# One decoder layer on one core: the attention's instructions in source order on every engine, and its output kept transposed up to W_o

## The chip, the cores and the metric

One core of a Trainium2 chip runs one program, from the inputs in HBM to the output in HBM. The metric is the device time of one execution in microseconds. TensorE (PE) multiplies, VectorE (DVE), ScalarE (ACT) and GpSimd (POOL) work on tiles, SyncE (SP) asks for transfers; each engine takes its own list of instructions, and semaphores hold one engine until another, or a transfer, is done.

## What is computed

One decoder layer over 1,024 rows of 1,024 columns, in float32. The mixer has two groups of eight heads, and their normed outputs go through W_o:

```python
z = hn @ w_in                                   # u, v, q, six k/v parts, gates
oa = u * (causal w_s applied to rms(v) per chunk of 128 + b_s)      # gMLP
o  = g0 * softmax(q kc) vc + g1 * softmax(q ks over 16 blocks) vs \
   + g2 * softmax(q kw in a window of 512) vw                       # NSA
h += concat([rmsnorm(oa), rmsnorm(o)]) @ w_o
h += hier_moe(rmsnorm(h))                       # 16 experts, 2 of 4 in the best group
h += (p @ w_ple_proj) * sigmoid(rmsnorm(h) @ w_ple_gate)
out = rmsnorm(h)
```

`rmsnorm(o)` divides each row of 512 numbers by its own root mean square; a factor per row may be applied before W_o or after it.

## The kernel before

The program runs through four stages. Up to about 230 us the projections of z are made; from there to about 617 us the attention runs; then come the routing and the experts, to 1,057 us; and then the last stage (PLE: the gate `pg`, the projection `pe`, the final norm). Products in full precision are made in three matmuls from a high and a low part of each operand (`th`/`tl`, `ph`/`pl`, `wh`/`wl`).

**The attention** is a loop over 132 slots; a slot is one tile of 128 keys for four heads and one block of 128 rows. `trans(s+1)` transposes the four probability tiles `P` of the next slot (L644), ACT copies them as `ph` (L650), DVE takes the rest as `pl` (L652). `run_later()` runs what was put off with `self.later(n, ...)`, above all the exponentials of a score bank (`exps`, L580). Then come matmuls of other work; then `score()` makes the scores of a coming bank (`S`, L565, two banks of PSUM), and DVE their row maxima (`nm`, L570); then `mult(s)` adds two matmuls to `O` (L669, L670). POOL scales `P` with the softmax's factor (L604) ahead of the transposes.

**The work between** is a generator: seven matmuls a slot of the last 96 products of `u` (L265) until the pool `late` is open, and after that about three a slot of W_o (`prod`, L771). When a group of 48 matmuls for two tiles of `u` is done, `evac_u` (L225 to L256) passes each tile through gelu, the mask product and a norm: ACT, POOL, DVE, ACT, POOL, DVE, ACT, POOL, and a store to `oa_scr` that POOL asks for (L255). `load_wo` (L740 to L749) brings 128 rows of W_o: two loads that SP asks for, `hi` on POOL (L748), `lo` on DVE (L749). The last four chunks of W_o pass through the one buffer each of `hT` and `hg`.

**What sets the order.** A scheduler lays out the program's instructions on each engine up to the line `self.manual.enter_context(tc.manual_schedule())`; after it they stand in the order in which the code issues them. In the kernel before that line stands behind the third `next(att)`, which runs the whole loop of slots, and the other work is handed to the scheduler with this:

```python
with self.tc.high_priority(offset=-100000), self.tc.issue_after(anchor[0].ins):
    while n < left:
        if next(work, None) is None:
            break
```

**The output of a block.** When a block of rows and four heads is through, ACT copies `O` (L674), PE transposes it in four pieces (L689), and DVE adds the two halves to `ob` (L690). When all eight heads are in, `attended` norms the block: the square on ACT, a factor of two small steps on POOL, and the scaling on DVE (L883). `half` transposes `ob` again for W_o in four pieces (L755).

Of the kernel before, what the change touches and what calls it, by code (L numbers as in the profile page):

```python
# [19 lines left out]
T = 1024  # L20
# [52 lines left out]
class K:  # L73
# [24 lines left out]
    def consts(self, pool):  # L98
# [6 lines left out]
        nc.vector.memset(self.neg_half, -0.5)  # L105
        self.idf = c[:, C_ID:C_ID + 128]
# [295 lines left out]
    def attention(self, blocks, done, work, count):  # L402
# [253 lines left out]
        def mult(s):  # L656
# [14 lines left out]
            if last:  # L671
                def copy(o=O[0]):
                    oe = sb.tile([128, 4, 128], F32, name="oe")
                    AC.activation(oe, o.rearrange("p (h q) -> p h q", h=4), AF.Copy)  # L674
                    if s + 1 < len(slots):
                        self.later(1, lambda: self.pq.append(lambda: out(i, g, oe)))
                    return oe

                if s + 1 < len(slots):
                    self.later(1, copy)  # L680
                else:
                    return i, g, copy()

        def out(i, g, oe):
            if g == 0:
                ob[i] = sb.tile([128, 512], F32, name="ob")
            tp = ps.tile([128, 4, 128], F32, name="tp")
# [16 lines left out]
        for s in range(len(slots)):  # L704
# [28 lines left out]
        out(*evac)  # L733
# [25 lines left out]
    def half(self, o):  # L759
# [3 lines left out]
        return th, tl  # L763

# [11 lines left out]
    def work(self, W, blocks):  # L776
# [31 lines left out]

        def add(X, n, p):
# [4 lines left out]
            V.tensor_add(X["h1"][:, s], p, X["h1"][:, s])  # L814
# [12 lines left out]
        def rest(X, nxt):  # L827
            trans_h(X, 1)
            load_h(nxt)
            self.logits(X["i"], X["hT"], X["hg"][:, T:T + 1])  # L830
# [9 lines left out]
        for n, i in enumerate(blocks[:-1]):  # L840
# [9 lines left out]
            X["ob"] = self.ready[i]  # L850
            trans(X, "ob")
            p = [None, None]
            for k in range(2):
                p[k] = ps.tile([128, 512], F32, name="wo", tag="fl")
                yield from self.prod(p[k], X["toa"], 0, k, True, False)
            trans(N, "oa")
            for k in range(2):
                yield from self.prod(p[k], X["tob"], 1, k, False, True)
                add(X, k, p[k])
# [13 lines left out]
    def attended(self, i, ob):  # L873
        def norm():
            sq = self.small.tile([128, 4], F32, name="sq")
            jk = self.sb.tile([128, 512], F32, name="junk", tag="ph")
            self.nc.scalar.activation(jk, ob, AF.Square, accum_out=sq[:, 0:1])
            self.rstd(sq[:, 1:2], sq[:, 0:1], 512)
            self.obs = sq

        def scale(self=self):
            sq = self.obs
            self.nc.vector.tensor_scalar(ob, ob, sq[:, 1:2], None, op0=OP.mult)  # L883

        def ready():
            self.ready[i] = ob

        norm()
        scale()
        ready()  # L890
# [36 lines left out]
    def tail(self, att, moe, work, i):  # L927
# [14 lines left out]
        for r in work:  # L942
            if r is None:
# [12 lines left out]
        tt = self.half(ob)  # L956
# [955 lines left out]
```

## Time and profile before

| | us |
|---|---|
| median of 3 runs | 1183.36 (1180.6 to 1183.68) |
| the profiled execution: its time | 1184.59 |
| its span, first to last instruction | 1182.9 |
| PE busy in the span | 1128.9 |
| DVE, ACT, POOL busy | 761.8, 664.6, 368.5 |

The profile is one execution. The 1.7 us between its time and its span lie around the span. Lines in it are those of the kernel before.

### The profile page before, as it was taken

To read this page: it belongs to the slowest core of one execution; us is meant where nothing else is said; L and a number is where in the kernel's file an instruction comes from. 1 tells how busy PE (TensorE), PEld (TensorE's weight loads), DVE (VectorE), ACT (ScalarE), POOL (GpSimd) and SP (SyncE) were. 2 spreads that over 40 slices of the span, in tenths; PEclk is the share of its full clock that TensorE was granted. 3 is DMA by queue.
4 is the path that set the end of the run, shared out by engine and by line. 5 is a ranking of instruction groups with operands and counts; after the bars stand their busy time and mean duration, and the time that the engine had idled before them with its cause. 6 is when DMAs were issued, how large, how long until landed. Compare 5 with 4: busy or idle time off the path is not lost. (4 is left out here: it accounts for less than half of the span.)

```text
span 1182.9 us, 17701 instructions
## 1 busy us (share of the span) xinstructions
PE 1128.9 (95%) x5969; PEld 862.6 (73%) x5969; DVE 761.8 (64%) x1264; ACT 664.6 (56%) x1295; POOL 368.5 (31%) x566
## 2 busy tenths in 40 slices
PE   7999999899899999999999989999999999997996
PEld 5798778777688888887775566766667776655885
DVE  4461144467877687767756568876777787646764
ACT  5562154467577777675643357665675665444433
POOL 1562242357533534433321120121112110012542
PEclk9999999999899999999999999999999999998999
DMA  7685241422530311330257797799768994674561
GB/s 271 203 214 145 66 136 59 155 70 69 192 125 5 108 63 42 98 116 5 79 200 257 290 333 252 248 366 416 284 217 293 410 362 162 197 273 171 187 215 70
DMA packets 75839, 219.54 MB, mean 186 GB/s; under 512 B 12777, under 2 KB 20329, under 8 KB 71137
## 3 DMA queue, kind: packets, MB, share of 16 engines
q1 hardware_dynamic: 63200, 177.68, 43.1%
q0 software_dynamic: 7792, 27.77, 7.4%
q10 hardware_dynamic: 4752, 12.93, 2.8%
q8 instruction: 48, 0.79, 0.3%
q14 instruction: 47, 0.38, 0.1%
HBM read 247.44 MB, written 40.11 MB: 243 GB/s over the span
## 5 line engine op out<-in xcount | busy, mean ns | idle before, releaser
L1413 DVE TENSOR_TENSOR wl<-ra,wh 128x1024 fp32r<-128x1024 f32 x192 | 232.1, 1237 | 54.6 <-ACT wh L1412 38.9
L1412 ACT ACTIVATE wh<-ra 128x1024 fp32r<-128x1024 f32 x176 | 180.3, 1056 | 68.5 <-PE y L91 41.0
L265 PE MATMUL z<-w,xh 128*128 128x512 f32 (+1 forms) x576 | 171.1, 379 | 8.1 <-ACT w L84 7.7
L604 POOL TENSOR_SCALAR P<-P,f 128x384 f32<-128x384 f32 (+3 forms) x188 | 105.1, 579 | 104.9 <-DVE f L625 61.9
L580 ACT ACTIVATE P<-S,nm 128x256 f32<-128x256 f32 (+3 forms) x192 | 105.3, 555 | 48.3 <-DVE nm L570 44.5
L265 PEld LDWEIGHTS z<-w,xh 128*128 128x128 f32 x576 | 105.1, 190 | 27.3 <-ACT w L84 7.7
L652 DVE TENSOR_TENSOR pl<-tp,ph 128x512 fp32r<-128x512 f32 x132 | 89.8, 685 | 39.0 <-ACT ph L650 38.3
L1410 POOL TENSOR_SCALAR wh<-ra 128x1024 fp32r<-128x1024 f32 x16 | 23.7, 1482 | 287.7 <-PE y L91 277.2
L89 PE MATMUL gu<-wh,mxh 128*128 128x512 f32 x256 | 108.3, 423 | 4.8 <-ACT wh L1412 4.8
L570 DVE TENSOR_REDUCE nm<-S 128x1 f32<-128x384 f32 (+3 forms) x148 | 91.6, 627 | 30.7 <-PE S L569 18.1
L265 PE MATMUL z<-w,xl 128*128 128x512 f32 (+1 forms) x288 | 109.0, 379 | 0.9 <-DVE xl L82 0.9
L90 PE MATMUL gu<-wl,mxh 128*128 128x512 f32 x256 | 101.7, 397 | 1.5 <-DVE wl L1413 1.5
L650 ACT ACTIVATE ph<-tp 128x512 fp32r<-128x512 f32 x132 | 78.2, 600 | 42.8 <-PE tp L644 42.2
L91 PE MATMUL gu<-wh,mxl 128*128 128x512 f32 x256 | 101.6, 397 | 0.0
L565 PE MATMUL S<-kT,qT 128*128 128x384 f32 (+3 forms) x384 | 92.6, 349 | 8.8 <-ACT P L580 6.6
L771 PE MATMUL wo<-wo,th 128*128 128x512 f32 x256 | 90.1, 425 | 0.0
L644 PE MATMUL tp<-c,P 128*128 128x128 f32 x528 | 83.5, 275 | 0.4 <-POOL P L604 0.4
L565 PEld LDWEIGHTS S<-kT,qT 128*128 128x128 f32 x384 | 62.9, 195 | 18.6 <-ACT P L580 9.4
L644 PEld LDWEIGHTS tp<-c,P 128*128 128x128 f32 x528 | 65.5, 142 | 12.3 <-POOL P L604 0.7
L89 PEld LDWEIGHTS gu<-wh,mxh 128*128 128x128 f32 x256 | 48.6, 190 | 30.0 <-ACT wh L1412 15.6
L265 PEld LDWEIGHTS z<-w,xl 128*128 128x128 f32 x288 | 54.7, 190 | 11.2 <-DVE xl L82 2.1
L670 PE MATMUL O<-pl,V 128*128 128x512 f32 x132 | 57.1, 433 | 1.0 <-DVE pl L652 1.0
(371 smaller groups left out, 2393.7 us busy)
## 6 DMA issues: line engine op xcount, KB each, us to landing
ra<-in_moe_w_gate SPq DMA_DIRECT2D x32, 1024.0 KB
ra<-in_moe_w_up SPq DMA_DIRECT2D x32, 1024.0 KB
ra<-in_moe_w_down SPq DMA_DIRECT2D x32, 1024.0 KB
rq<-in_moe_w_gate SPq DMA_DIRECT2D x40, 512.0 KB
rq<-in_moe_w_up SPq DMA_DIRECT2D x40, 512.0 KB
rq<-in_moe_w_down SPq DMA_DIRECT2D x40, 512.0 KB
y_scr<-yo ACTq DMA_DIRECT2D x19, 512.0 KB
wraw<-in_w_in SPq DMA_DIRECT2D x32, 256.0 KB
```

What stands on the lines that cost most here:

```text
L89: mm(out, xh, wh, start=first, stop=False)
L90: mm(out, xh, wl, start=False, stop=False)
L91: mm(out, xl, wh, start=False, stop=last)
L265: self.nc.tensor.matmul(p[:, :n], x, w, start=(cc == 0 and j == 0), stop=(cc == 7 and j == 2))
L565: PE.matmul(S[:, x], qT[i, g][:, h0 + x, a], kk, start=(x + a == 0), stop=(x == hp - 1 and a == 1 and not (dm or wm)))
L570: V.tensor_reduce(u["nm"][:, h0:h0 + hp, k], S, axis=AX.X, op=OP.max, negate=True)
L580: AC.activation(u["P"][k][:, h], S[:, x], AF.Exp, bias=u["nm"][:, h, k:k + 1], accum_out=u["l"][:, h, k:k + 1])
L604: e.tensor_scalar(P, P, f[:, h, k:k + 1], 1.0, op0=OP.mult, op1=OP.mult)
L644: anchor[0] = PE.transpose(tp[:, h], u["P"][k][:, h, kb * 128:(kb + 1) * 128], self.idf)
L771: self.nc.tensor.matmul(p, x, w[:, s], start=first and k + a == 0, stop=last and k == 3 and a == 2)
L1412: AC.activation(hi, w, AF.Copy)
L1413: V.tensor_tensor(lo, w, raw(hi), op=OP.subtract)
```

## The change

1. `tc.manual_schedule()` is entered ahead of the third `next(att)`, and the priority and the anchor are gone. The loop of slots with its other work then stands in the order of the code on all five engines.
2. `O` stays transposed. ACT copies half of it (64 partitions, L685 of the changed kernel), and DVE makes two sums of 64x256 (L687); the four transposes of `O`, the reduction and the four transposes of `ob` are gone. The norm is taken from the square of the transposed block by four matmuls with a column of ones (`norm_t`, `norm_sum`), and its factor is applied after W_o (`add`); the part from `oa` is added on its own (`add_a`).
3. Some steps are put off by a slot (`later`), and the tail calls `tick` more often.
4. In the last stage the gather of the first rows is asked for first, all projections stand ahead of the first transposes, and the other gathers wait for the first rows. The experts' last store is one transfer on ACT's queue.

```diff
@@ mult, out
             if last:
-                def copy(o=O[0]):
-                    oe = sb.tile([128, 4, 128], F32, name="oe")
-                    AC.activation(oe, o.rearrange("p (h q) -> p h q", h=4), AF.Copy)
-                    if s + 1 < len(slots):
-                        self.later(1, lambda: self.pq.append(lambda: out(i, g, oe)))
-                    return oe
...
+                f = lambda o=O[0]: out(i, g, o.rearrange("p (h q) -> p h q", h=4))
                 if s + 1 < len(slots):
-                    self.later(1, copy)
+                    self.later(1, f)
...
-            for h in range(4):
-                PE.transpose(tp[:, h], oe[:, h], self.idf)
-            V.tensor_reduce(ob[i][:, g * 256:(g + 1) * 256].rearrange("p (h d) -> p h d", h=4),
-                            tp.rearrange("p h (a d) -> p h d a", a=2), axis=AX.X, op=OP.add)
+            oe = sb.tile([64, 4, 128], F32, name="oe")
+            AC.activation(oe, o[64:128], AF.Copy)
+            for k in range(2):
+                V.tensor_tensor(ob[i][k * 64:(k + 1) * 64, 2 * g:2 * g + 2], o[0:64, k:4:2], oe[:, k:4:2], op=OP.add)
@@ the loop of slots
-            with self.tc.high_priority(offset=-100000), self.tc.issue_after(anchor[0].ins):
-                while n < left:
-                    if next(work, None) is None:
-                        break
-                    count[0] -= 1
-                    n += 1
+            while n < left:
+                if next(work, None) is None:
+                    break
+                count[0] -= 1
+                n += 1
@@ the norm
+    def norm_t(self, dst, jk, o, tag):
+        self.nc.scalar.activation(jk, o.rearrange("p c q -> p (c q)"), AF.Square)
+        return lambda: self.norm_sum(dst, jk, tag)
+
+    def norm_sum(self, dst, jk, tag):
+        nc = self.nc
+        r = self.ps.tile([128, 512], F32, name="nt", tag=tag)
+        for c in range(4):
+            nc.tensor.matmul(r[:, 0:1], jk[:, c * 128:(c + 1) * 128], self.one, start=(c == 0), stop=(c == 3))
+        nc.vector.tensor_scalar(dst, r[:, 0:1], 1.0 / 512, EPS, op0=OP.mult, op1=OP.add)
+        nc.gpsimd.tensor_tensor(dst, dst, self.neg_half, op=OP.pow)
@@ the W_o work
-            V.tensor_add(X["h1"][:, s], p, X["h1"][:, s])
+            V.scalar_tensor_tensor(X["h1"][:, s], p, X["rb"], X["h1"][:, s], op0=OP.mult, op1=OP.add)
...
-            X["ob"] = self.ready[i]
-            trans(X, "ob")
-            p = [None, None]
+            X["ob"], X["rb"] = self.ready[i]
+            X["tob"] = self.half_t(X["ob"])
...
                 if k == 0:
-                    trans_h(X, 0)
+                    self.later(1, lambda X=X: trans_h(X, 0))
                 else:
-                    rest(X, N)
+                    self.later(1, *rest(X, N))
@@ mixer
             self.open_late = open_late
+            self.manual.enter_context(tc.manual_schedule())
             next(att)
-            self.manual.enter_context(tc.manual_schedule())
@@ last stage
             load_h(tiles[0], nc.sync)
+            load_y(0)
...
-            for q in range(4):
+            for q in range(NP):
                 proj(q)
-            for c in range(1, 3):
-                part(c)
-
+
+                if q < 4:
+                    part(q + 1)
+                if q >= 4:
+                    AC.activation(*late.pop(0), AF.Copy)
+                if q == 3:
+                    add_y(0)
+            trans(tiles[0])
+
+            G.tensor_copy(sb.tile([128, 8], F32, name="sq")[:, 0:1], tiles[0]["y"][1][:, 0:1])
             load_h(tiles[1], G)
```

The order on DVE where the second group of `u` is through and the last four chunks of W_o come in (`wo_3042`, `wo_3051`, `wo6_3060`, `wo7_3069`; `pl`, `nm` and `f` belong to slots). Before, from the middle of it:

```order
L749 SCALAR_TENSOR_TENSOR wo_3051<-hT_3052,par_71,wo_3051 128x512
L570 TENSOR_REDUCE nm_3357<-S_3440 128x1
L749 SCALAR_TENSOR_TENSOR wo_3051<-hg_3056,par_71,wo_3051 128x512
L652 TENSOR_TENSOR pl_3284<-tp_3278,ph_3283 128x512
L608 RECIPROCAL f0_3457<-l_3358 128x4
L652 TENSOR_TENSOR pl_3304<-tp_3298,ph_3303 128x512
L609 TENSOR_TENSOR f_3456<-f0_3457,gates_85 128x4
L749 SCALAR_TENSOR_TENSOR wo6_3060<-hT_3061,par_71,wo6_3060 128x512
L570 TENSOR_REDUCE nm_3472<-S_3474 128x1
L652 TENSOR_TENSOR pl_3324<-tp_3318,ph_3323 128x512
L570 TENSOR_REDUCE nm_3472<-S_3479 128x1
L749 SCALAR_TENSOR_TENSOR wo6_3060<-hg_3065,par_71,wo6_3060 128x512
```

And now, from the first of its eight `lo` steps on (L744 is L749 of before, L572 is L570):

```order
L744 SCALAR_TENSOR_TENSOR wo_3042<-hT_3043,par_71,wo_3042 128x512
L744 SCALAR_TENSOR_TENSOR wo_3042<-hg_3047,par_71,wo_3042 128x512
L744 SCALAR_TENSOR_TENSOR wo_3051<-hT_3052,par_71,wo_3051 128x512
L744 SCALAR_TENSOR_TENSOR wo_3051<-hg_3056,par_71,wo_3051 128x512
L744 SCALAR_TENSOR_TENSOR wo6_3060<-hT_3061,par_71,wo6_3060 128x512
L744 SCALAR_TENSOR_TENSOR wo6_3060<-hg_3065,par_71,wo6_3060 128x512
L744 SCALAR_TENSOR_TENSOR wo7_3069<-hT_3070,par_71,wo7_3069 128x512
L744 SCALAR_TENSOR_TENSOR wo7_3069<-hg_3074,par_71,wo7_3069 128x512
L1111 TENSOR_TENSOR rt_3080<-rt_3080,par_71 128x160
L82 TENSOR_TENSOR tl_3086<-tp4_3087,th_3085 128x512
L82 TENSOR_TENSOR tl_3100<-ob_2621,th_3099 128x512
L572 TENSOR_REDUCE nm_2959<-S_3106 128x1
```

Before, steps of slots stand between any two chunks of W_o; now the eight steps of four chunks, the router's weights and two `tl` stand in a row, and the first `nm` of a slot behind them.

The order on POOL at the same place: `sv` and `ev` belong to `evac_u`, P is scaled for the slots. Before:

```order
L95 TENSOR_SCALAR sv_3013<-sv_3013 128x1
L96 TENSOR_TENSOR sv_3013<-sv_3013,neg_half_73 128x1
L254 TENSOR_SCALAR ev_2999<-ev_2999,sv_3013 128x512
L255 DMA oa_scr_65<-ev_2999 128x512
L244 TENSOR_TENSOR e_3020<-ev_3001 128x512
L247 TENSOR_TENSOR ev_3001<-ev_3001,M_3011 128x512
L604 TENSOR_SCALAR P_2270<-P_2270,f_2977 128x384 x4
L95 TENSOR_SCALAR sv_3026<-sv_3026 128x1
L96 TENSOR_TENSOR sv_3026<-sv_3026,neg_half_73 128x1
L254 TENSOR_SCALAR ev_3001<-ev_3001,sv_3026 128x512
L255 DMA oa_scr_65<-ev_3001 128x512
L506 TENSOR_TENSOR Pc_3156<-Pc_3156,lc_3190 128x2x4x64
```

And now (L606 is L604 of before, L257 is L255, L743 is L748):

```order
L95 TENSOR_SCALAR sv_3013<-sv_3013 128x1
L96 TENSOR_TENSOR sv_3013<-sv_3013,neg_half_73 128x1
L256 TENSOR_SCALAR ev_2999<-ev_2999,sv_3013 128x512
L257 DMA oa_scr_65<-ev_2999 128x512
L246 TENSOR_TENSOR e_3020<-ev_3001 128x512
L249 TENSOR_TENSOR ev_3001<-ev_3001,M_3011 128x512
L95 TENSOR_SCALAR sv_3026<-sv_3026 128x1
L96 TENSOR_TENSOR sv_3026<-sv_3026,neg_half_73 128x1
L256 TENSOR_SCALAR ev_3001<-ev_3001,sv_3026 128x512
L257 DMA oa_scr_65<-ev_3001 128x512
L743 TENSOR_SCALAR wo_3042<-hT_3043,par_71 128x512
L743 TENSOR_SCALAR wo_3042<-hg_3047,par_71 128x512
```

Before, P is scaled between the steps of two tiles; now the steps of the second tile begin behind the store of the first, and eight `hi` steps follow (the first two are shown), ahead of the next scaling of P.

The order on PE at that place. Before, ahead of the first products with W_o:

```order
L569 MATMUL S<-mb,idb 128x128
L755 MATMUL tp_3087<-c,oa 128x128 x4
L755 MATMUL tp_3101<-c,ob 128x128
L644 MATMUL tp<-c,P 128x128 x4
L755 MATMUL tp_3101<-c,ob 128x128 x3
L565 MATMUL S<-kT,qT 128x512 x2
L569 LDWEIGHTS idb
L569 MATMUL S<-mb,idb 128x128
L565 MATMUL S<-kT,qT 128x512 x2
L569 LDWEIGHTS idb
L569 MATMUL S<-mb,idb 128x128
L771 MATMUL wo<-wo,th 128x512 x2
```

And now, from the row behind the last product of `u` on (L786 is L771 of before, L567 is L565, L646 is L644):

```order
L750 MATMUL tp_3087<-c,oa 128x128 x4
L786 MATMUL wo<-wo,th 128x512 x2
L567 MATMUL S<-kT,qT 128x512 x2
L571 LDWEIGHTS idb
L571 MATMUL S<-mb,idb 128x128
L671 MATMUL O<-ph,V 128x512
L672 MATMUL O<-pl,V 128x512
L646 MATMUL tp<-c,P 128x128 x4
L485 LDWEIGHTS idb
L485 MATMUL S<-mc,idb 128x512
L489 MATMUL S<-kcT,qT 128x64 x16
L786 MATMUL wo<-wo,tl 128x512
```

Now the first two products with `th` stand ahead of one bank of scores, and the first product with `tl` ahead of all scores that follow, where before six banks of scores (the last two are shown) stood ahead of the products.

## Rows read from the trace of the kernel before

**Rows 1.** the page, part 1: busy time, share, instructions of each engine
```profile
PE 1128.9 (95%) x5969; PEld 862.6 (73%) x5969; DVE 761.8 (64%) x1264; ACT 664.6 (56%) x1295; POOL 368.5 (31%) x566
```

**Rows 2.** stretches of the core: us, busy time of each engine, granted clock, DMA share, GB/s
```profile
240.00:270.00 30.00, 29.02 (x171) 23.82 (x171) 20.70 (x41) 18.78 (x51) 18.26 (x31) 0.97 0.19 59
270.00:300.00 30.00, 28.85 (x170) 22.82 (x169) 23.62 (x42) 21.57 (x54) 21.67 (x32) 1.00 0.27 88
300.00:330.00 30.00, 27.72 (x147) 21.22 (x148) 23.58 (x43) 18.24 (x43) 16.87 (x25) 0.89 0.52 174
303.20:310.00 6.80, 6.35 (x23) 4.67 (x23) 4.62 (x9) 4.23 (x11) 5.06 (x7) 0.50 0.99 295
330.00:360.00 30.00, 30.00 (x199) 25.76 (x198) 22.62 (x48) 20.05 (x50) 10.99 (x16) 1.00 0.35 111
540.00:570.00 30.00, 29.03 (x170) 22.68 (x169) 23.88 (x48) 19.06 (x51) 11.01 (x16) 1.00 0.14 45
```

**Rows 3.** the page, part 5: PE's scores, with the idle time before them
```profile
L565 PE MATMUL S<-kT,qT 128*128 128x384 f32 (+3 forms) x384 | 92.6, 349 | 8.8 <-ACT P L580 6.6
```

**Rows 4.** timeline of POOL, one tile of u: start, us, instruction [idle before]
```profile
294.35 1.03 POOL L244 TENSOR_TENSOR e<-ev 128x512 f32<-128x512 f32 x1 [0.29 <-ACT ev L232]
296.38 1.27 POOL L247 TENSOR_TENSOR ev<-ev,M 128x512 f32<-128x512 f32 x1 [0.99 <-DVE e L245]
297.77 2.73 POOL L604 TENSOR_SCALAR P<-P,f 128x384 f32<-128x384 f32 x4
300.59 0.19 POOL L95 TENSOR_SCALAR sv<-sv 128x1 f32<-128x1 f32 x1
302.51 0.61 POOL L255 DMA_DIRECT2D oa_scr<-ev  x1 [0.30 <-POOL ev L254]
```

**Rows 5.** groups by line and form, 200 to 640 us: busy, mean ns
```profile
L248 DVE SCALAR_TENSOR_TENSOR ev<-e,ev 128x512 f32<-128x512 f32 x4 | 3.1, 775 | 0.1
L252 ACT ACTIVATE jk<-ev 128x512 bf16<-128x512 f32 x8 | 5.1, 634 | 9.2 <-DVE ev L240 5.9 <-DVE ev L248 3.2
```

**Rows 6.** a load of W_o: SP's and POOL's timeline, and a group of DVE
```profile
320.06 0.33 SPq L745 DMA_DIRECT2D hT<-in_w_o  x1
322.60 0.69 POOL L748 TENSOR_SCALAR wo<-hT,par 128x512 fp32r<-128x512 f32 x1 [3.68 <-DMA hT<-in_w_o]
L749 DVE SCALAR_TENSOR_TENSOR wo<-hT,par,wo 128x512 fp32r<-128x512 f32 x4 | 3.0, 743 | 0.0
```

**Rows 7.** groups of a slot, 200 to 640 us, and PE's timeline
```profile
L650 ACT ACTIVATE ph<-tp 128x512 fp32r<-128x512 f32 x132 | 78.2, 600 | 42.8 <-PE tp L644 42.2
L580 ACT ACTIVATE P<-S,nm 128x512 f32<-128x512 f32 x48 | 32.9, 689 | 19.4 <-DVE nm L570 17.3 <-DVE lc L503 1.7 <-PE tp L644 0.2
L580 ACT ACTIVATION_READ_ACCUMULATOR P<-S,nm 128x1 f32 x192 | 39.2, 204 | 0.0
L570 DVE TENSOR_REDUCE nm<-S 128x1 f32<-128x512 f32 x48 | 32.5, 683 | 6.5 <-PE S L565 3.8 <-PE S L569 2.5
1079.04 0.39 PE L91 MATMUL pg<-pgh,tl 128*128 128x512 f32 x1
1079.27 0.40 PE L89 MATMUL pg<-pgh,th 128*128 128x512 f32 x1
```

**Rows 8.** timeline of PE: small transposes and matmuls
```profile
427.47 0.60 PE L689 MATMUL tp<-c,oe 128*128 128x128 f32 x4
567.49 0.97 PE L896 MATMUL ro<-rt,hT 128*128 128x20 f32 x8
```

**Rows 9.** timeline of PE and DVE at the start of the last stage
```profile
1058.41 7.11 PE L1741 MATMUL pe<-rb 128*128 128x512 f32 x16 [0.89 <-DVEq L1615]
1068.29 2.81 DVE L1671 SCALAR_TENSOR_TENSOR h<-yg,wt,h 128x512 f32<-128x512 f32 x4 [2.07 <-DMA yg<-y_scr,slot]
1070.54 1.94 PE L1680 MATMUL tp<-c,h 128*128 128x128 f32 x8 [5.02 <-issue]
1072.27 6.46 PE L1741 MATMUL pe<-rb 128*128 128x512 f32 x12
```

More of the change, by code (lines that the diff above doesn't have):

```diff
@@ L105, in consts @@
         nc.vector.memset(self.neg_half, -0.5)
+        self.one = pool.tile([128, 1], F32, name="one")
+        nc.vector.memset(self.one, 1.0)
         self.idf = c[:, C_ID:C_ID + 128]
@@ L732, in attention @@
         yield
-        out(*evac)
+        evac()
     def load_wo(self, c, pool, tag=None):
@@ L763, in half, with half_t @@
         return th, tl
+    def half_t(self, o):
+        th = self.late.tile([128, 4, 128], F32R, name="th", bufs=2)
+        tl = self.late.tile([128, 4, 128], F32R, name="tl", bufs=2)
+        self.split(th, tl, o)
+        return th, tl
+    def norm_t(self, dst, jk, o, tag):
[8 more added lines that the diff above has]
+        nc.gpsimd.tensor_tensor(dst, dst, self.neg_half, op=OP.pow)
     def prod(self, p, tt, b, n, first, last):
@@ L827, in rest, with one @@
         def rest(X, nxt):
-            trans_h(X, 1)
-            load_h(nxt)
-            self.logits(X["i"], X["hT"], X["hg"][:, T:T + 1])
+            def one():
+                trans_h(X, 1)
+                load_h(nxt)
+            return one, lambda: self.logits(X["i"], X["hT"], X["hg"][:, T:T + 1])
         for i, X in M.items():
@@ L873, in attended @@
     def attended(self, i, ob):
[L874 to L883, printed above, removed]
+        sq = self.small.tile([128, 4], F32, name="sq")
+        f = []
         def ready():
[L886 to L890, printed above, removed]
+            self.ready[i] = ob, sq[:, 1:2]
+        self.later(1, lambda: f.append(self.norm_t(sq[:, 1:2], self.sb.tile([128, 512], F32, name="junk", tag="ph"), ob, "tp")),
+                   lambda: f[0](), ready)
     def logits(self, i, hT, scale):
@@ L941, in tail @@
         self.moe_start()
-        for r in work:
-            if r is None:
+        for k, r in enumerate(work):
+            if r is None or k % 3 == 2:
                 self.tick()
@@ L955, in tail @@
         ob = self.ob
-        tt = self.half(ob)
-        AC.activation(hg[:, :512], ob, AF.Square, accum_out=sq[:, 0:1])
-        self.rstd(sq[:, 1:2], sq[:, 0:1], 512)
+        tt = self.half_t(ob)
+        norm = self.norm_t(sq[:, 1:2], hg[:, :512], ob, "tp")
         fill(4)
@@ L964, in tail @@
             for k, _ in enumerate(self.prod(p, tt, 1, n, True, True)):
+                if n == 0 and k == 5:
+                    norm()
                 if n and k == 6:
@@ L1043, in mixer @@
                 self.small = Slots(**{k: [(sm, 4)] for k in ("nm", "l", "f", "f0", "nmc", "lc", "sq")})
+                self.small.add("sq", [(sm, 8)])
                 self.wo, self.wo_todo, self.wo_open = {}, [], []
@@ L1730, in ple @@
             part(0)
-            load_y(0)
             pT, pw = self.late_p
@@ L1757, in ple @@
             G.dma_start(gf, A["norm_final"].to_broadcast([128, T]))
-            add_y(0)
-            trans(tiles[0])
             parts(tiles[0])
-            for q in range(4, NP):
-                proj(q)
-            for c in range(3, 8):
+            for c in range(5, 8):
                 part(c)
-                if c in (3, 4, 6):
-                    AC.activation(*late.pop(0), AF.Copy)
             norm(tiles[0])
```

23 lines of the change are left out of this document (13 added, 10 removed).

## The prediction

> **What bounds the kernel now.** I read the page first: PE is busy 1128.9 us of 1182.9 [rows 1], so the kernel is bound by PE, and a change is worth what it takes from PE's work, from its idle time, or from the time at half clock. A share over four stages says little, so I went on to stretches of 30 us through the attention, which is what the change rewrites [rows 2]. The reader is to see two things. From 330 to 600 us PE is busy 30.00 of 30 in most stretches; of the nine, two fall short, the larger by 0.97 and the other by 0.46, so 1.4 us is all that a better order could win there. And from 240 to 330 us PE loses 0.98 + 1.15 + 2.28 = 4.4 us idle; the granted clock of 0.97 and 0.89 costs another 0.03 x 30 + 0.11 x 30 = 4.2 us, and the row inside shows what that is: 6.8 us at 0.50, which is 1.2 GHz of 2.4, right after an idle gap. Together 8.6 us: in that stretch the two groups of `u` are passed on and W_o comes in. Then the scores' row: their wait is put down to ACT's exponentials in 6.6 of 8.8 us [rows 3], so the first thing that runs late when DVE or ACT are held up is a bank of scores.
>
> So the order before already hides nearly everything. The question is what the order of the code leaves open, and that is read from the order by following each engine's list at the places where something long stands in a row.
>
> **Part 1, the order: two blockades.** When 48 products of `u` are done, two tiles go through `evac_u`. In the new order POOL has the second tile's steps behind the first one's store, and DVE has both tiles' steps, then the `lo` steps of W_o, and only then the next `nm` and `pl`. For one tile the trace shows, on POOL, 294.35 to 297.65 for the first two steps, and 300.59 to 303.12 for the last ones with the request of the store; between them stand 2.73 us of scaling P [rows 4], which the new order puts elsewhere, and one step of DVE and one of ACT, 0.78 + 0.63 = 1.4 [rows 5]. So one tile takes 3.3 + 1.4 + 2.5 = 7.2 us, and two in a row 14.5 us; it can't be under 8.8 - 2.7 = 6.0 each.
>
> One chunk of W_o after that: from SP's request to POOL's start are 322.60 - 320.06 = 2.54 us, `hi` takes 0.69 and `lo` 0.74 [rows 6]. The two halves of a chunk are loaded together, and a half's buffer is free only when its `lo` is done, so each chunk that finds no free buffer costs a round of 2.54 + 0.69 + 0.74 = 4.0 us; the second half trails the first by 0.7.
>
> First blockade (slot 6): 14.5 us for two tiles, 2 x 0.69 + 0.74 = 2.1 for the chunk that is there, 4.0 + 0.7 for the next, and two `nm` of 0.68 [rows 7] before an exponential can free a bank: 22.7 us after the last product of `u`. What PE still has in its own list up to the bank that waits is the rest of a slot and seven products of the next, some twenty matmuls of 0.23 (the step from one start to the next, 1079.04 to 1079.27 [rows 7]): 5 us. **Idle: 18 us.** Second blockade (slot 13): 14.5 us, 2.1 for the first of four chunks, three rounds of 4.0, the router's weights and `tl` at about 1 us: 29.6 us, plus some 0.05 to 0.1 at each of a score of hand-overs, 30.5. In that time PE's list holds four transposes, two products with `th`, a bank of scores, two matmuls on `O`, four transposes and sixteen small scores with their mask: about 4.5 us at 0.23 a wide and 0.11 a small one (below). **Idle: 26 us.**
>
> The nearest rows say that PE comes out of such a gap at half clock, 6.8 us at 0.50 [rows 2], so 3.4 us each time if work is there at once: I take 5 us for both, between 0 and 6.8. The 8.6 us that are lost there today are inside these figures and come off. Net: 18 + 26 + 5 - 8.6 = **+40 us**. The low bound takes 6.0 us a tile (-5), no half clock (-5) and loads that are half hidden by POOL's own work (-6): +24. The high one takes the other load of the same kind, 3.7 us instead of 2.5 (-> +5), and all of the half clock: +47.
>
> A rule speaks to this place. The Trainium skill, "PSUM — Partial Sum Buffer", section "Engine vs sequencer instructions", says that the queues of ScalarE, VectorE and GpSimdE are strictly first in, first out, and that matmuls start and complete in program order. By it nothing behind a waiting `lo` step can pass it, on any of the four engines, as the sum above has it; were there passing, the sum would be that of the second rival.
>
> **Part 1, the steady slots.** In the new order a slot's scores stand in the slot itself, behind three products with W_o. Where a slot asks for two banks (21 of the 117 from slot 14 on, counted in the order), the second bank is free when the exponentials of this very slot are through, and these stand behind `ph` on ACT: 0.60 + 0.69 + 0.20 = 1.49 us from the end of the transposes [rows 7], with two of them 2.4. PE covers three products of 0.23, or these and one bank (0.56): 0.7 to 1.3 us. That leaves 0.2 to 1.1 us; at 0.65 each 14 us, less the 1.4 that are lost there today: **+12 us** (bounds 0, where the loop has the work of a slot before in hand, and 23). DVE gets 14 more additions and 32 sums of half the size for 16 reductions and 7 scalings: at 0.68 for 512 columns [rows 7] some 5 us more; it has no row over 24 of 30 [rows 2], so its idle time hides them, and without that cover it would be the 5 us.
>
> **Part 2, transposed output.** PE loses 16 x 4 transposes of `O` and 8 x 4 of `ob`. Four take 0.60 us and one 0.27, so one step is 0.11; the small router matmuls, eight in 0.97, are the row nearest to the one-column matmuls, 0.10 each [rows 8]. So -96 x 0.11 + 32 x 0.10 = **-7 us** (bounds -10.6 if the new ones cost nothing, -3 if each costs a lone matmul's 0.23). The copies of ACT change little, and the reductions of DVE become two sums.
>
> **Part 4, the last stage.** Now PE makes four projections, from 1058.41 to 1065.52, then waits 5.02 us for DVE, whose additions of the gathered rows begin at 1068.29; then come transposes, and three projections that take 6.46 us at half clock, up to 1078.7 [rows 9]. With all seven projections first (28 matmuls at 7.11 / 16 = 0.44: 12.4 us, to 1070.9) the wait is covered, and the first gate products begin near 1074 instead of 1078.2: **-4 us** (bounds 0 and -5.0). Part 3 and the one store on ACT's queue I cost at nothing: the steps that are put off lie beside a slot's matmuls, the store beside the projections; uncovered, a step of ACT's is 0.60 us [rows 7].
>
> **The sum.** 1184.6 + 40 + 12 - 7 - 4 = 1225.6 for a profiled execution; the median of the runs shown is 1.2 below that of before, so **1224 us**. Its own range, with the bounds above, is 1210 to 1238.
>
> **The rivals.** *Cheaper blockades.* Part of the chain of the second tile runs beside the first's, and loads lie beside it: +24 instead of +40 and half of the slots' waits: 1224 - 16 - 6 = 1202. For it: PE's list is not empty at the start of either gap, and the gap of today is small with the same steps. Against: the rows of POOL stand strictly one tile behind the other. *Nothing is blocked* (the other side). If the code's order only leaves what the 4.4 us idle show today, since W_o's chunks come before they are needed, parts 2 and 4 remain: 1183.4 - 7 - 4 = 1172. It decides if the added idle stays under 11 us; for it speaks that PE idles so little now with all the same steps on the same engines; against it that the first `nm` stands behind eight `lo` steps. Between 11 and 18 us lies the case with no change to speak of, 1180 to 1187. *Dearer.* The late start lets banks, `P` and the stats of a unit run late for more slots, and the wait in the steady slots is at its bound of 23: 1250.
>
> A price that only a page has: the Trainium skill, "DMA: Bandwidth & Descriptors", "Latency and other measured facts", lets a request to HBM take 0.2 us on average and 2 us at high load. The row of 2.54 us lies above both, and the load share is 0.52 there; by the light figure the rounds would shrink and the forecast come nearer to the first rival.
>
> **How the numbers follow.** Forecast 0.58, cheaper 0.18, dearer 0.10, nothing blocked 0.09, in between 0.05. A measurement of this kernel can tell about 0.3% from no change, that is 1179.8 to 1186.9. Faster takes the third rival's 0.09; the same 0.03 of the case in between; slower the rest, 0.88. The range reaches from 1196, below the cheaper case, to 1244, within the dearer: it leaves out 0.09 + 0.05 and about half of 0.10.
>
> **What would show it.** Right: two gaps of PE of some 15 to 30 us near 250 and 300 us, which end in `lo` steps of DVE and loads of W_o, each with a stretch at 0.50 behind it; waits of scores on ACT of some 15 us over the later slots; no transposes of `O`; and the first gate product 4 us sooner after the last expert's matmul. Wrong: if PE's list holds enough work at the two places, or if another engine's list has the slot's steps ahead of the long chains; then PE stays busy from 240 to 330 us, and the time is below that of before.

## The result and the profile after

| | before | after |
|---|---|---|
| median, us | 1183.52 (4 runs) | 1351.05 (1342.87 to 1354.95, 4 runs) |
| ratio | | 1.1406, 95% interval 1.137 to 1.1442 |
| span of the profiled execution, us | 1182.9 | 1353.2 |
| first scores to the last transposes of P, us | 232.4 to 614.7: 382.3 | 232.3 to 786.7: 554.4 |
| last stage, first projection to the end, us | 1058.4 to 1182.9: 124.5 | 1230.1 to 1353.2: 123.1 |

The direction is that of the forecast, the size is four times as large: +168 us where +41 was forecast. All of it lies in the attention; what lies between it and the last stage is 443.5 us after and 443.7 before. The profiled execution of the changed kernel is the slowest of its four runs.

The page of the changed kernel, part 1, answers to [rows 1]:

```profile
PE 1184.6 (88%) x5937; PEld 897.1 (66%) x5937; DVE 776.1 (57%) x1296; ACT 666.1 (49%) x1287; POOL 364.7 (27%) x559
```

PE is 56 us longer busy than before, with fewer instructions, and 115 us longer idle. The stretches of [rows 2], and the attention as a whole, in the changed kernel (columns as there):

```profile
240.00:270.00 30.00, 27.01 (x148) 22.65 (x149) 17.88 (x39) 16.66 (x49) 13.55 (x25) 0.90 0.08 26
270.00:300.00 30.00, 10.48 (x54) 7.63 (x53) 10.68 (x18) 8.34 (x21) 11.87 (x16) 0.73 0.21 70
300.00:330.00 30.00, 20.97 (x117) 16.78 (x116) 10.55 (x20) 12.79 (x31) 9.39 (x15) 0.90 0.10 32
330.00:360.00 30.00, 9.17 (x37) 6.32 (x35) 10.80 (x17) 4.33 (x9) 11.61 (x18) 0.56 0.49 158
540.00:570.00 30.00, 26.02 (x155) 21.26 (x153) 16.72 (x36) 16.93 (x45) 10.81 (x20) 0.94 0.30 97
232.30:786.70 554.40, 429.79 (x2277) 342.88 (x2278) 286.84 (x594) 257.32 (x669) 172.03 (x276) 0.85 0.18 57
```

Two things are to be seen. From 270 to 360 us PE stands for about half of the time; these are the two blockades of the forecast. But a stretch far behind them, 540 to 570 us, where [rows 2] have 29.03 of 30 busy at a clock of 1.00, has 26.02 at 0.94, and the clock over the whole attention is 0.85. Split where the transposes of P for slot 16 start, behind both blockades (before, then changed kernel):

```profile
232.44:310.81 78.37, 70.29 (x391) 55.47 (x392) 55.64 (x103) 51.41 (x134) 51.73 (x80) 0.93 0.33 103
310.81:614.73 303.92, 302.27 (x1914) 252.82 (x1913) 220.61 (x463) 203.83 (x541) 120.97 (x203) 1.00 0.25 82
232.33:362.47 130.14, 73.89 (x375) 58.16 (x376) 55.50 (x104) 46.80 (x121) 50.97 (x80) 0.76 0.23 76
362.47:786.67 424.20, 355.87 (x1902) 284.68 (x1901) 231.34 (x492) 210.52 (x548) 121.03 (x196) 0.88 0.16 51
```

The part up to slot 16 is 52 us longer. The part behind it is 120 us longer, and PE is idle there for 68.3 us instead of 1.6.

What PE waited for, first up to 360 us and then from there to 800 us (us in total, times, the longest):

```profile
PE S L567 <- ACT P L582: 20.6, 2, 19.0
PE wo L786 <- DVE tl L82: 16.2, 1, 16.2
PE tp L750 <- DMA oa<-oa_scr: 8.3, 1, 8.3
PE wo L786 <- ACT th L81: 4.6, 1, 4.6
```

```profile
PE S L567 <- ACT P L582: 31.9, 20, 7.5
PE O L665 <- DVE ob L687: 12.6, 9, 2.6
PE O L672 <- DVE pl L654: 6.5, 2, 5.5
PE ro L910 <- ACT qT L480: 5.2, 1, 5.2
PE tp L513 <- POOL Pc L508: 3.6, 1, 3.6
```

The first list is the blockades: 19.0 us in one wait for a bank, then 8.3, 4.6 and 16.2 us. The four rounds of W_o are there as worked out (DVE, changed kernel, start, us, instruction; the `lo` steps of `hg` in between are left out):

```profile
338.11 1.17 DVE L744 SCALAR_TENSOR_TENSOR wo<-hT,par,wo 128x512 fp32r<-128x512 f32 x1 [4.16 <-POOL wo L743]
343.16 1.17 DVE L744 SCALAR_TENSOR_TENSOR wo<-hT,par,wo 128x512 fp32r<-128x512 f32 x1 [3.21 <-POOL wo L743]
347.77 0.75 DVE L744 SCALAR_TENSOR_TENSOR wo<-hT,par,wo 128x512 fp32r<-128x512 f32 x1 [2.77 <-POOL wo L743]
352.25 0.75 DVE L744 SCALAR_TENSOR_TENSOR wo<-hT,par,wo 128x512 fp32r<-128x512 f32 x1 [2.38 <-POOL wo L743]
356.29 0.68 DVE L82 TENSOR_TENSOR tl<-tp,th 128x512 fp32r<-128x512 f32 x1
```

The steps from one `lo` of `hT` to the next are 5.05, 4.61 and 4.48 us, 4.0 forecast. The second list holds two things that the forecast did not have. One is a wait of ACT:

```profile
420.49 0.60 ACT L840 ACTIVATE hT<-tp 128x512 f32<-128x512 f32 x1 [0.71 <-PE tp L750]
427.19 1.06 ACT L842 ACTIVATE jk<-h 128x1024 bf16<-128x1024 f32 x1 [6.10 <-DMA y_scr<-oa]
428.24 0.46 ACT L582 ACTIVATE P<-S,nm 128x256 f32<-128x256 f32 x1
```

```profile
420.19 1.26 SPq L866 DMA_DIRECT2D y_scr<-oa  x2
421.55 1.19 SPq L815 DMA_DIRECT2D oa<-oa_scr  x1
```

The square of `h1` writes into `jk`, which takes turns with `oa` in two buffers, and the buffer is being read by two stores to `y_scr` that SP has asked for at 420.19. ACT waits 6.10 us, the exponentials stand behind it, and PE's bank of scores comes 7.5 us late. Over 360 to 800 us ACT waits so six times, 29.1 us. The other is O: it has one bank of PSUM, and the next block's first product waits until DVE's two sums have read it, 12.6 us in nine places.

The half clock is a third thing. The 16 stretches of the attention in which the granted clock was 0.50, in four rows and their sum:

```profile
341.90:372.60 30.70, 11.70 (x33) 8.08 (x34) 13.67 (x24) 3.87 (x8) 7.67 (x11) 0.50 0.40 127
...
423.80:440.80 17.00, 11.51 (x43) 9.90 (x44) 2.88 (x7) 5.16 (x15) 0.74 (x2) 0.50 0.42 113
...
536.40:539.80 3.40, 3.40 (x13) 2.94 (x12) 3.26 (x9) 1.35 (x3) 1.66 (x2) 0.50 0.02 5
...
724.10:737.80 13.70, 12.80 (x42) 10.89 (x43) 3.42 (x6) 4.57 (x13) 0.74 (x2) 0.50 0.26 78
sum 163.80, PE 105.53 PEld 87.03 DVE 58.72 ACT 50.13 POOL 41.12; mean PE 6.60 PEld 5.44 DVE 3.67 ACT 3.13 POOL 2.57
```

PE worked 105.5 us at 0.50, which full speed would have done in half of that: 52.8 us lost, against 4.7 before (9.4 us of work at 0.50). Each of the 16 stretches begins inside an idle gap of PE or within 4 us behind one; the gap at the stretch from 423.8 is 7.5 us, the one ahead of 536.4 is 1.8, and the shortest, ahead of 758.3, 0.7. Behind the two blockades it is the three stretches from 283.8 to 372.6 us, with 3.0, 4.2 and 11.7 us of PE's work; the twelve behind them hold 78.2 us. So the 172 us of the attention are 115 us idle, 48 of half clock, and 9 that I can't assign. The half clock differs from run to run: the four runs of the changed kernel go from 1342.87 us at a mean granted clock of 0.942 to 1354.95 us at 0.930.

### The profile page after: what moved, and what is told of

It reads as the page before. It is cut to its first block, busy times and chain, and to the rows that moved or that the text cites. A ratio compares the mean times of both kernels' runs of the same rounds, so it can differ in the third digit from the quotient of the medians.

```text
span 1353.2 us, 17685 instructions
## 1 busy us (share of the span) xinstructions
PE 1184.6 (88%) x5937; PEld 897.1 (66%) x5937; DVE 776.1 (57%) x1296; ACT 666.1 (49%) x1287; POOL 364.7 (27%) x559
## 5 line engine op out<-in xcount | busy, mean ns | idle before, releaser
L1429 DVE TENSOR_TENSOR wl<-ra,wh 128x1024 fp32r<-128x1024 f32 x192 | 235.5, 1258 | 49.9 <-ACT wh L1428 39.4
L606 POOL TENSOR_SCALAR P<-P,f 128x256 f32<-128x256 f32 (+3 forms) x188 | 104.3, 577 | 184.0 <-DVE f L627 73.6
L567 PE MATMUL S<-kT,qT 128*128 128x384 f32 (+3 forms) x384 | 100.2, 371 | 58.5 <-ACT P L582 55.7
L567 PEld LDWEIGHTS S<-kT,qT 128*128 128x128 f32 x384 | 69.0, 210 | 81.3 <-ACT P L582 68.2
L572 DVE TENSOR_REDUCE nm<-S 128x1 f32<-128x384 f32 (+3 forms) x148 | 91.6, 627 | 49.1 <-PE S L571 24.5
L786 PE MATMUL wo<-wo,th 128*128 128x512 f32 x256 | 99.4, 470 | 4.6 <-ACT th L81 4.6
L1426 POOL TENSOR_SCALAR wh<-ra 128x1024 fp32r<-128x1024 f32 x16 | 18.8, 1178 | 283.2 <-PE y L91 272.8
L646 PE MATMUL tp<-c,P 128*128 128x128 f32 x528 | 88.4, 293 | 2.9 <-POOL P L606 2.4
L646 PEld LDWEIGHTS tp<-c,P 128*128 128x128 f32 x528 | 73.1, 153 | 25.3 <-issue 4.6
L786 PE MATMUL wo<-wo,tl 128*128 128x512 f32 x128 | 54.2, 424 | 16.2 <-DVE tl L82 16.2
L671 PE MATMUL O<-ph,V 128*128 128x512 f32 x132 | 64.7, 490 | 0.0
```

Of the source, the lines that this page charges most:

```text
L567: PE.matmul(S[:, x], qT[i, g][:, h0 + x, a], kk, start=(x + a == 0), stop=(x == hp - 1 and a == 1 and not (dm or wm)))
L572: V.tensor_reduce(u["nm"][:, h0:h0 + hp, k], S, axis=AX.X, op=OP.max, negate=True)
L606: e.tensor_scalar(P, P, f[:, h, k:k + 1], 1.0, op0=OP.mult, op1=OP.mult)
L646: anchor[0] = PE.transpose(tp[:, h], u["P"][k][:, h, kb * 128:(kb + 1) * 128], self.idf)
L786: self.nc.tensor.matmul(p, x, w[:, s], start=first and k + a == 0, stop=last and k == 3 and a == 2)
L1429: V.tensor_tensor(lo, w, raw(hi), op=OP.subtract)
```

## The experiments

Two theories. **Theory 1:** the order does it, by long work that stands in a row on an engine's list, and by the half clock behind each gap. **Theory 2**, its rival: the transposed output does a large part, through O's one bank and the longer chain of the norm. Times are medians of two runs, of ten for e2 and e5, of twelve for e11, of four for the changed kernel; PE's idle time and its work at half clock are of the attention, first scores to last transposes of P.

| run | us | attention | PE idle | PE's work at 0.50 |
|---|---|---|---|---|
| before | 1183.5 | 382.3 | 9.7 | 9.4 |
| changed kernel | 1351.1 | 554.3 | 124.6 | 105.6 |
| e1, order alone | 1356.2 | 552.2 | 118.8 | 106.7 |
| e2, all but the order | 1185.5 | 389.2 | 12.5 | 18.9 |
| e5, e2 with O freed by ACT | 1186.4 | 387.5 | 13.1 | 13.9 |
| e11, last stage alone | 1181.4 | 382.2 | 9.7 | 9.2 |
| e3, jk elsewhere | 1312.6 | 507.2 | 99.7 | 59.0 |
| e4, O freed by ACT | 1344.4 | 543.1 | 124.3 | 79.5 |
| e6, W_o spread | 1338.3 | 541.0 | 110.3 | 109.3 |
| e7, waits spread | 1273.4 | 467.9 | 65.6 | 46.5 |
| e8, e7 with two banks of O | 1283.8 | 482.9 | 70.2 | 64.8 |
| e10, e7 with O ahead of S | 1255.6 | 455.2 | 58.5 | 48.1 |
| e9, order from slot 16 | 1290.4 | 488.6 | 78.1 | 65.7 |
| e9b, e9 with jk elsewhere | 1255.6 | 453.5 | 53.9 | 44.2 |

**The order alone.** The kernel before with part 1:

```diff
-            with self.tc.high_priority(offset=-100000), self.tc.issue_after(anchor[0].ins):
-                while n < left:
...
+            while n < left:
...
+            self.manual.enter_context(tc.manual_schedule())
             next(att)
-            self.manual.enter_context(tc.manual_schedule())
```

> The kernel before with part 1 of the change alone: the loop of slots stands in the order of the code, the priority and the anchor are gone, the output is still copied, transposed and scaled as before. Theory 1 (the order does it: PE's idle time and the half clock that follows its gaps): 1320 to 1350 us, PE idle some 160 us, PE busy some 55 us above the kernel before. Theory 2 (the transposed output does a large part, since two sums of DVE now hold O's one bank and the norm's chain is longer): under 1280 us.

1356.21 us, ratio 1.1487 (1.1464 to 1.151): as long as the changed kernel, and 6 us above theory 1's range. The waits differ in part: the stores don't hold ACT here, but PE waits for the sums of `h1` before it may transpose them, which part 3 of the change puts off by a slot; and O, which one copy of ACT frees here, holds PE for 6.1 us, where the changed kernel has 14.1 over the whole attention:

```profile
PE S L565 <- ACT P L580: 34.3, 23, 18.6
PE tp L754 <- DVE h L813: 21.7, 7, 4.4
PE O L663 <- ACT oe L674: 6.1, 6, 2.7
```

So part 1 is enough for the whole loss, and theory 2 is out as the main cause. It doesn't follow that each wait of the changed kernel belongs to part 1 alone: the wait for the stores stands neither in this run's trace nor in that of the next run, which has all but the order; it takes both, and which part of the rest brings it is not tested.

**All but the order.** The changed kernel with the diff of part 1 taken back:

```diff
+            with self.tc.high_priority(offset=-100000), self.tc.issue_after(anchor[0].ins):
+                while n < left:
...
-            self.manual.enter_context(tc.manual_schedule())
             next(att)
+            self.manual.enter_context(tc.manual_schedule())
```

> The changed kernel without part 1: the loop of slots is laid out by the scheduler again, with the priority and the anchor, and all the rest of the change (transposed output, steps put off, last stage) stays. Theory 1: 1170 to 1180 us, since the terms of -7 (96 transposes for 32 narrow matmuls) and -4 (last stage) are left. Theory 2: well above 1190 us.

1185.54 us, ratio 1.0013 (0.9993 to 1.0034), no change that can be told. Both theories missed: the order is the cause, but the gain of the rest, 11 us in the forecast, does not reach the time. Outside the attention this run is 4.7 us shorter than the kernel before in the profiles, 3.4 between attention and last stage and 1.3 in the last stage; the attention takes that back. One part of it was counted wrongly. The one-column matmuls (changed kernel, by tile):

```profile
L776 PE MATMUL nt<-one,junk x56: 169/250/250, 308.6 to 715.3; 128*128 128x1 f32 x56
L776 PE MATMUL nt<-one,hg x8: 166/250/250, 800.8 to 801.5; 128*128 128x1 f32 x8
```

These are 64, not 32: each of these float32 matmuls of the code runs as two (the small router matmuls of [rows 8] do so too: 128 in the group of before for 64 in the code). In this run eight end 0.95 us after the first starts, so the term is -96 x 0.11 + 64 x 0.10 = -4 us instead of -7. The attention was 6.9 us longer all the same: 2.8 us more idle, and 9.5 us more work at 0.50, which is 4.7 us. DVE works 11.8 us more in this run (773.6 for 761.8), where the forecast had some 5; whether that lengthens the attention is not shown.

**Is it O's bank, there?** ACT copies both halves, so that O is free after two copies:

```diff
             AC.activation(oe, o[64:128], AF.Copy)
+            of = sb.tile([64, 4, 128], F32, name="of", tag="ph")
+            AC.activation(of, o[0:64], AF.Copy)
             for k in range(2):
-                V.tensor_tensor(ob[i][k * 64:(k + 1) * 64, 2 * g:2 * g + 2], o[0:64, k:4:2], oe[:, k:4:2], op=OP.add)
+                V.tensor_tensor(ob[i][k * 64:(k + 1) * 64, 2 * g:2 * g + 2], of[:, k:4:2], oe[:, k:4:2], op=OP.add)
```

> The run with part 1 taken out again (the scheduler lays out the slots, all the rest of the change stays), with O's one bank freed by two copies of ACT instead of by DVE's two sums. With part 1 out, the attention was still 7 us longer than in the kernel before, where I had counted 7 us less. If that is O's bank, which before was free after one copy: 1172 to 1179 us. If it is chance of the layout, or the longer chain of the norm: 1182 to 1190 us.

1186.41 us, ratio 1.0011 (0.9991 to 1.0032). Not O's bank. Why the scheduler's layout of the transposed output saves no time stays open.

**The last stage alone**, part 4 in the kernel before (its core; the rest of part 4 as in the diff ahead of the prediction):

```diff
+            load_y(0)
...
-            for q in range(4):
+            for q in range(NP):
                 proj(q)
...
-            for s in (slice(0, 512), slice(512, T)):
-                nc.sync.dma_start(self.y_scr[B["t"] * 128:(B["t"] + 1) * 128, s], o[:, s])
+            nc.scalar.dma_start(self.y_scr[B["t"] * 128:(B["t"] + 1) * 128], o)
```

> The kernel before with part 4 of the change alone: the last stage and the one store on ACT's queue. If the last stage gives the 4 us that I forecast: 1178 to 1181 us. If it gives what the last stage of the changed kernel shows (123.1 us from the first projection to the end, 124.5 before): about 1182.5 us, within what can be told from no change. Rival (the store on ACT's queue costs the gather its start): above 1184 us.

1181.37 us, ratio 0.9984 (0.9965 to 1.0003): not clear of no change, and the interval's end, 4.1 us less, just takes in the forecast. The last stage takes 124.1 us in its profile, 124.5 before; by the profile, then, the 4 us are not there.

**The stores behind ACT's wait.** In the changed kernel:

```diff
-                AC.activation(sb.tile([128, T], BF, name="jk", tag="oa", bufs=2), X["h1"], AF.Square, accum_out=X["sq"][:, 0:1])
+                AC.activation(self.sb.tile([128, T], BF, name="jk", tag="ph"), X["h1"], AF.Square, accum_out=X["sq"][:, 0:1])
```

> The changed kernel, where the square of h1 goes into a buffer that no store reads (that of ph) and not into one of the two of oa, which the stores of filler rows to y_scr read. In the trace of the changed kernel ACT waits six times for such a store, 29.1 us in all. Theory 1: these waits are gone from PE with the half clock behind them, 1300 to 1325 us. Rival: the slots then wait for the next thing in the row (the store's buffer is wanted by the next load of oa), 1345 to 1355 us.

1312.57 us, 38 less. The attention is 47 us shorter: 25 us less idle and (105.6 - 59.0) / 2 = 23 us less half clock. ACT's wait of 29.1 us thus cost nearly as much in clock as in idle time. The 47 us are those of the two profiled executions, the slowest of four and the faster of two; the medians differ by 38.

**O's bank in source order**, the diff of the two copies above in the changed kernel:

> The changed kernel, where ACT copies both halves of O, so that O's one bank is free after two copies (1.2 us) and does not wait for DVE's two sums. PE waits 14.1 us in 11 places for these sums. If that wait matters: 1325 to 1340 us. Rival: the second copy (16 x 0.6 us) on ACT takes back what the bank gives, 1345 to 1360 us.

1344.39 us, 7 less than the changed kernel's median and between the two ranges, but within the spread of that kernel's own four runs (1342.87 to 1354.95): no gain is shown. PE now waits 10.3 us for ACT's second copy instead of 14.1 us for DVE. Idle is the same; work at 0.50 is 26 us less, which the idle time does not explain.

**W_o spread.** Each of the last four chunks is asked for in one slot and split in the next, one chunk every two slots:

```diff
-                for c in range(4, 6):
-                    self.load_wo(c, self.sb, "xt")
-                for c in range(6, 8):
-                    self.load_wo(c, wp)
+                for c in range(4, 8):
+                    self.later(1 + 2 * (c - 4), *(self.load_wo(c, self.sb, "xt", True) if c < 6 else self.load_wo(c, wp, None, True)))
```

> The changed kernel, where the last four chunks of W_o are asked for in one slot and split in the next, one chunk every two slots, instead of all in one go. Theory 1 (four rounds of a load in a row hold DVE's list, and with it PE): the wait for tl, 16.2 us, is gone, and some of the half clock behind it: 1325 to 1338 us. Rival (the tl waits for the evac of u anyway, and the loads' rounds turn up in the next slots): 1345 to 1355 us.

1338.27 us (1333.19 to 1343.35), 13 less by the medians and 0.3 above theory 1's range; the slower run lies within the spread of the changed kernel. The trace is clearer: the wait for `tl`, 16.2 us, is gone from PE's list, and idle falls by 14.3. The work at 0.50 does not fall, so the second half of theory 1's price did not come off here.

**All waits that were found, spread or moved.** This run has W_o spread as above in both places, `jk` elsewhere, O freed by ACT, and the steps of `evac_u` one a slot, the longest (`two`) cut in two; the products of W_o wait until they are through:

```diff
-            for k in (a, e, b, c, f, d, g, h):
+            for k in (a, e, b):
                 k()
...
+            left = [*c, d, f, *g, h]
+            if t2 < 3:
+                for x in range(2 * t2 - 2, 2 * t2):
+                    left += self.load_wo(x, self.sb, "xs", True)
+            self.later(1, *left)
```

> The changed kernel in source order with all found waits spread or moved: the steps of evac_u one a slot, W_o's chunks one every two slots, the square of h1 in another buffer, O freed by two copies of ACT. The products of W_o begin some slots later. Theory 1 (the order as such costs nothing, it is what stands in a row in it): PE's idle time in the attention falls from 125 to some 50 us, and its busy time with it to some 395: 1235 to 1270 us. Rival (source order costs in every slot): above 1290 us.

1273.35 us (1269.06 to 1277.64), just above the range of theory 1. Against the changed kernel 59 us of idle and 30 us of half clock are gone, but 56 us of idle above the kernel before are left, and no wait in the list is long any more:

```profile
PE S L571 <- ACT P L586: 19.0, 22, 3.3
PE O L669 <- ACT of L691: 13.7, 12, 2.2
PE O L676 <- DVE pl L658: 8.5, 4, 5.6
PE tp L517 <- POOL Pc L512: 6.3, 1, 6.3
```

**Two banks of O** in that run, with one copy again; the bank is taken from the three of `tp`:

```diff
-                self.ps = Slots(tp=[(pm, 3)], z=[(pz, 3)])
+                self.ps = Slots(tp=[(pm, 2)], z=[(pz, 3)])
...
-            self.ps.add("O", [(pl, 1)])
+            self.ps.add("O", [(pl, 2)])
```

> The run with the waits spread, with O in two banks of PSUM (and the bank taken from the three of tp), and the single copy of the change again. In the run with the waits spread PE still waits 13.7 us in 12 places for O's one bank. Theory 1: this and the half clock behind it go, 1250 to 1262 us. Rival: with two banks of tp the transposes wait instead, 1270 to 1285 us.

1283.78 us: the rival. O's wait is out of the list; the transposes wait instead (0.9 and 6.3 us on the same two lines in the run with the waits spread):

```profile
PE tp L483 <- DVE pl L658: 8.0, 7, 1.8
PE tp L517 <- POOL Pc L512: 7.8, 1, 7.8
```

**O ahead of the scores** in the run with the waits spread: 

```diff
+            evac = mult(s)
             for n in range(2):
                 b = state["bank"]
...
                     score()
-            evac = mult(s)
```

> The run with the waits spread, where the two matmuls on O stand ahead of the scores in each slot instead of behind them, 0.46 us more of work ahead of a bank that waits. Theory 1 (a bank's wait in a slot with two banks is exp behind ph on ACT, less what PE has ahead of it): the 19 us of waits for exponentials fall to some 9, 1255 to 1265 us. Rival (the matmuls on O wait for pl themselves, and the wait only moves): 1268 to 1280 us.

1255.61 us, 18 less, as theory 1 has it: the waits of scores fell from 19.0 us in 22 places to 9.6 in 12. The idle time fell by 7.1 us only, as the waits for `pl` and O grew; what else made the run shorter stays open.

```profile
PE O L669 <- ACT of L691: 14.7, 12, 3.0
PE O L676 <- DVE pl L658: 10.9, 4, 5.1
PE S L571 <- ACT P L586: 9.6, 12, 3.2
```

**Source order from slot 16 on**, behind both blockades; the scheduler has the slots ahead of it:

```diff
         for s in range(len(slots)):
             self.now = s
+            if s == 16:
+                self.manual.enter_context(self.tc.manual_schedule())
...
+            with ExitStack() as z:
+                if s < 16:
+                    z.enter_context(self.tc.high_priority(offset=-100000))
+                    z.enter_context(self.tc.issue_after(anchor[0].ins))
```

> The changed kernel, where the scheduler lays out slots 0 to 15 with the priority and the anchor of before, and source order begins at slot 16, behind the two places where u is passed on and W_o comes in. Theory 1: the two blockades and the half clock behind them go, some 53 + 20 us, and the steady slots keep their loss: 1265 to 1290 us. Rival (the steady slots lose only because they start late): under 1220 us.

> The same, with the square of h1 in another buffer than that of oa. Theory 1: the 38 us that this took off the changed kernel come off here too: 1228 to 1252 us. Rival (the waits for the stores come from the blockades, which shift the stores): no change against the run without it.

1290.44 us for the first, 0.4 above theory 1's range: the two blockades, with whatever else the first sixteen slots lost, are worth 554.3 - 488.6 = 66 us of the attention. From slot 16 on:

```profile
304.08:720.59 416.51, 345.32 (x1908) 275.56 (x1908) 237.41 (x499) 210.62 (x548) 127.14 (x205) 0.92 0.20 63
```

PE is idle there for 71.2 us, against 68.3 in the changed kernel, so what the later slots wait for does not come from a late start. 1255.55 us for the second, 35 less, close to the 38 that it took off the changed kernel, though above the range of 1228 to 1252: the waits for the stores don't come from the blockades. With both gone the attention is still 71 us longer than before; its longest waits:

```profile
PE S L567 <- ACT P L582: 18.1, 22, 3.3
PE O L665 <- DVE ob L687: 13.0, 9, 2.5
PE O L672 <- DVE pl L654: 7.0, 2, 5.9
PE tp L646 <- POOL P L606: 3.0, 7, 0.7
```

No version beat the kernel before beyond what can be told.

## Why the prediction was wrong, step by step

**What bounds the kernel: right.** PE does, and before the change it was idle 9.7 us in the attention. **The two blockades: right in place and nearly in size.** "Idle: 18 us" was one wait of 19.0; "Idle: 26 us" was 8.3 + 4.6 + 16.2 = 29.1, though the forecast had it as one wait that ends with `tl`, and PE stood first for the load of `oa` and for `th`. The rule drawn on, first in, first out on the three engines (the Trainium skill, "PSUM — Partial Sum Buffer", "Engine vs sequencer instructions"), agrees with the trace: on DVE nothing passed the `lo` steps between 338 and 356 us. Up to slot 16 the attention is 52 us longer, where the forecast had 40 and at most 47.

**The half clock: mis-sized behind the blockades, and left out everywhere else.** Behind the two blockades I took 5 us, at most 6.8, by one row of 6.8 us at 0.50; in the three stretches there PE worked 18.9 us at 0.50, which is 9.5 us lost. For the gaps of the steady slots I took nothing; the twelve stretches there hold 78.2 us of work, 39 us lost, since the half clock came back behind later gaps of 0.7 to 7.5 us (behind many of under 1 us it didn't), and since one stretch can be long: from 423.8 it lasts 17.0 us, with 11.5 of work. The Trainium skill, "TensorE: Matmul & The Clock Gate", "HAM oscillation — how this bites in real kernels", has this: bursts of matmuls with waits between them start slow again and again. The trace agrees, with 105.5 us of PE's work at 0.50, and it shows more: nine of the 16 stretches have a gap of 3.2 us or more at their start, the other seven only gaps of 0.7 to 2.6 us ahead of them.

**The steady slots: the step that failed.** From slot 16 on "+12 us" was forecast, and measured are 424.2 - 303.9 = 120. The 12 us were one mechanism alone, a second bank in a slot. That mechanism is there and of that size: in e9b PE waits 18.1 us in 22 places for exponentials, 14.4 us in 20 places of it behind the start of slot 16 (14 us in 21 slots were forecast), and in e10 0.46 us more of work ahead of the bank halves the wait. But I went through one wait and costed the rest of the order at nothing. Missing were the wait of ACT for the stores (47 us of the attention by e3, 35 by e9b against e9), which comes only with the order and the rest of the change together, and which a look at who reads `jk`'s two buffers would have shown; O's one bank, 12.6 us of waits, which the change itself makes longer, as two sums of DVE stand where one copy of ACT freed it (6.1 us in e1); and small waits for `pl` and P. Half clock came with them: of the 106 us that are left in e9, 68 are idle and 28 are half clock. Taken off one after the other the 172 us are 66 (e9), 35 (e9b) and 71 that are left, of which 44 are idle, 17 half clock and 10 not assigned. No run takes the waits that are left off one by one. The bound of 23 us was worked out for the one wait, so the range could not reach: with every bound at its high end the sum is 1184.6 + 47 + 23 - 3 - 0 - 1.2 = 1250 us (and 1192 at the low ends, so that "1210 to 1238" is narrower than its own bounds).

**Transposed output: sign of the work right, count wrong.** 64 one-column matmuls, not 32, so -4 instead of -7, and even that is not seen in the time (e2, e5). **Last stage:** the covered wait of 5.02 us is gone as forecast, and the first gate product comes 13.8 us behind the first projection instead of 19.8, 5.9 us sooner where 4 was forecast. But the stage is only 1.4 us shorter, and in e11 0.4. PE stands longer ahead of the second rows' transposes (before, then changed kernel):

```profile
1085.24 1.07 PE L1680 MATMUL tp<-c,h 128*128 128x128 f32 x8 [1.03 <-DVE h L1671]
1243.96 0.50 PE L89 MATMUL pg<-pgh,th 128*128 128x512 f32 x1
1252.50 1.28 PE L1695 MATMUL tp<-c,h 128*128 128x128 f32 x8 [2.39 <-DVE h L1686]
```

That is 1.4 us; 3.4 us at 0.50 behind it cost 1.7 more, and the next five tiles take 12.0 us each instead of 11.8. The forecast stopped at the first gate product and did not follow what comes behind it.

**Rivals.** "Nothing is blocked" fell with the first wait. "Dearer" was the right direction, at 1250 us, but for the wrong reason: in e9 the later slots don't start late, and PE is idle in them as long.

## What to carry to other kernels

When an order is taken from a scheduler and given to the source, go through the whole loop engine by engine and list for every instruction the last reader of the buffer that it writes, scratch buffers and transfers included; each is a wait that the scheduler may have been hiding, and a forecast that prices one of them prices none of the others. On a kernel bound by PE add to the gaps the work at half clock that follows them: here 48 us on top of 115. Long chains (a norm, a round of loads) belong one step a slot in such an order; with the scratch output moved and O copied out by ACT it took 78 us off here, and the result was still 90 us from what the scheduler had found, 72 with the products on O ahead of the scores.

## What the hardware showed that I had not expected

A float32 matmul of one column, or of twenty, ran as two instructions of about 0.1 us each: 64 one-column matmuls for 32 in the code, 128 of twenty columns for 64. And the half clock came behind short gaps too: the stretch at 0.50 from 536.4 us began 0.5 us behind a gap of 1.8 us. One stretch has no gap ahead of it: in e2 3.4 us at 0.50 from 445.3 us, with PE busy for 40 us before. What PE ran just ahead of it were narrow matmuls, eight of one column and fourteen of twenty; no run tests whether these brought the half clock:

```profile
441.72 0.95 PE L777 MATMUL nt<-one,junk 128*128 128x1 f32 x8
443.32 1.63 PE L911 MATMUL ro<-rt,hT 128*128 128x20 f32 x14
```
